# Splitting the first load of a DMA-bound rotation kernel into 2 KB and 62 KB of each row

## Chip, cores and metric

One core of a Trainium2 chip. The metric is the time of one execution on the device in microseconds (us).

## The reference

```python
def reference(x):                       # x: (32, 3, 256, 256) float32
    return np.rot90(x, k=2, axes=(-2, -1)).astype(np.float32)
```

Each of 96 images of 256 x 256 elements is turned by 180 degrees: as a row of 65,536 elements, it is reversed. 25.17 MB are read and 25.17 MB written, and nothing is computed.

## The kernel before

An image is cut into four rows of 16,384 elements (64 KB), and 32 images make a tile of 128 partitions, 8 MB. Three tiles (A, Bt, Ct) hold everything. VectorE mirrors each row in place through a scratch tile T, and the store puts the four rows of an image in reverse order. All transfers are issued on SyncE's one queue.

```python
E = L // 4                  # 16384 elements, 64 KB
J = E // 8
# ... x4, o4: views of input and output; A, Bt, Ct: [128, E]; T: [128, J]

def load(t, g, lo, hi):
    return nc.sync.dma_start(out=t[:, lo:hi], in_=x4[g][:, lo:hi])

def inside(t):
    for lo in range(0, E // 2, J):
        hi = E - lo - J
        copy(T[:, :], back(t, hi, hi + J))
        copy(t[:, hi:hi + J], back(t, lo, lo + J))
        copy(t[:, lo:lo + J], T[:, :])

TAIL = 1536
load(A, 0, 0, E)
load(Bt, 1, 0, E)
body = load(Ct, 2, 0, E - TAIL)
load(Ct, 2, E - TAIL, E)
inside(A)
first = store(A, 0)         # made to wait for `body`: queued while the last strip is on its way
# ... cut: the dependency of `first` on `body`
for g, t in ((1, Bt), (2, Ct)):
    inside(t)
    store(t, g)
```

Of the kernel before, what the change touches and what calls it, by code (L numbers as in the profile page):

```python
# [2 lines left out]

os.environ.setdefault("NEURON_RT_ULTRASERVER_MODE", "4")

# [4 lines left out]


@with_exitstack
def kernel(
    ctx: ExitStack,
    tc: tile.TileContext,
    x: bass.AP,
    out: bass.AP,
):








    nc = tc.nc
    P = 128

    B, C, H, W = x.shape
    L = H * W
    G = 32
    E = L // 4
    J = E // 8

    x4 = x.rearrange("b c h w -> (b c) (h w)").rearrange(
        "(g n) (s e) -> g (n s) e", n=G, s=4)
    o4 = out.rearrange("b c h w -> (b c) (h w)").rearrange(
        "(g n) (s e) -> g n s e", n=G, s=4)  # L40

    pool = ctx.enter_context(tc.tile_pool(name="slots", bufs=1))
    A = pool.tile([P, E], x.dtype, tag="A")
    Bt = pool.tile([P, E], x.dtype, tag="B")
    Ct = pool.tile([P, E], x.dtype, tag="C")
    T = pool.tile([P, J], x.dtype, tag="T")

    def back(t, lo, hi):
        return t[:, hi - 1:(lo - 1 if lo else None):-1]

    def copy(dst, src):
        tc.keep_in_program_order(nc.vector.tensor_copy(out=dst, in_=src))  # L52

    def load(t, g, lo, hi):
        return nc.sync.dma_start(out=t[:, lo:hi], in_=x4[g][:, lo:hi])  # L55

    def store(t, g):
        return nc.sync.dma_start(out=o4[g][:, ::-1, :], in_=t[:, :])
# [6 lines that stand above are left out]
            copy(t[:, lo:lo + J], T[:, :])  # L65

    TAIL = 1536
    load(A, 0, 0, E)
    load(Bt, 1, 0, E)
    body = load(Ct, 2, 0, E - TAIL)  # L70
    load(Ct, 2, E - TAIL, E)
    inside(A)
    first = store(A, 0)
    tc.add_manual_dep(
        first.ins, body.ins.name,
        mybir.DependencyInfo(mybir.DependencyClass.Sync, mybir.DependencyReason.DATA),
        reason="the first store is queued while the last strip is on its way")
# [5 lines that stand above are left out]
# [1 line left out]
_INS = ['x']  # L84
_OUTS = [((32, 3, 256, 256), 'float32')]


# [23 lines left out]
```

## Time and profile before

| | before |
|---|---|
| time, first 3 runs | 122.18 us median (122.0 to 122.47) |
| span of the program in the trace | 120.2 us |
| DMA queue busy | 97.3% |
| VectorE busy | 37% |

The span is shorter than the time by about 1.8 us that lie outside the program. The steady pace is 2.418 us for a row of 64 KB on one of the 16 DMA engines; each engine takes eight rows of a tile, and each row is one packet in the trace. The start is the stretch from the first issue at 0.73 us until all engines run at that pace. The prediction shows the lines.

### The profile page before, as it was taken

The page shows a single profiled execution, that of the slowest core. Times are in us where ns is not written, and L with a number is a line of the kernel's source. Part 1 is how long each engine was busy: PE and PEld are TensorE (multiplying, and loading weights), DVE is VectorE, ACT ScalarE, POOL GpSimd, SP SyncE. Part 2 cuts the span into 40 slices and gives each one's busy share as a digit, 9 for nine tenths or more (in the row PEclk, how much of TensorE's full clock was granted, in tenths as well). Part 3 has the DMA queues.
Part 4 walks back from the last instruction along what each step waited for, and adds up shares of the span by engine and source line. Part 5 has one row for each costly group of instructions (what it writes and reads, how often), then busy time and mean ns, then how long its engine had stood idle before and what let it go on. Part 6 is the DMA issues. An engine that isn't in the chain of part 4 may idle for free.

```text
span 120.2 us, 93 instructions
## 1 busy us (share of the span) xinstructions
DVE 44.2 (37%) x36; POOL 0.2 (0%) x4
## 2 busy tenths in 40 slices
DVE  0000000499995099999059999400000000000000
POOL 0000000000000000000000000000000000000000
DMA  9888988898889779779499888988898889888990
GB/s 349 349 349 371 676 349 349 371 676 349 349 349 698 316 316 632 316 336 613 202 408 698 349 349 349 698 349 349 349 698 349 349 349 698 349 349 349 632 414 0
DMA packets 1008, 50.33 MB, mean 419 GB/s; under 512 B 112, under 2 KB 112, under 8 KB 240
## 3 DMA queue, kind: packets, MB, share of 16 engines
q1 hardware_dynamic: 1008, 50.33, 97.3%
HBM read 25.17 MB, written 25.17 MB: 419 GB/s over the span
## 4 chain that ended last, share of the span: by engine, by line
DMA 34%; DVE 25%; another core or an unknown queue 4%; issue 1%; SPq 0%; DVEq 0%
DMA Bt<-in_x_dram 34%; DVE T L52 8%; DVE Bt L52 8%; DVE Ct L52 8%; SPq L55 0%; DVEq L52 0%
## 5 line engine op out<-in xcount | busy, mean ns | idle before, releaser
L52 DVE COPY T<-A 128x2048 f32<-128x2048 f32 x4 | 4.9, 1227 | 22.6 <-DMA A<-in_x_dram 22.5
L52 DVE COPY T<-Ct 128x2048 f32<-128x2048 f32 x4 | 4.9, 1227 | 4.5 <-DMA Ct<-in_x_dram 4.4
L52 DVE COPY T<-Bt 128x2048 f32<-128x2048 f32 x4 | 4.9, 1227 | 4.4 <-DMA Bt<-in_x_dram 4.3
L52 DVE COPY Bt<-T 128x2048 f32<-128x2048 f32 x4 | 4.9, 1227 | 0.1
L52 DVE COPY A<-T 128x2048 f32<-128x2048 f32 x4 | 4.9, 1227 | 0.1
L52 DVE COPY Ct<-T 128x2048 f32<-128x2048 f32 x4 | 4.9, 1227 | 0.1
L52 DVE COPY A<-A 128x2048 f32<-128x2048 f32 x4 | 4.9, 1227 | 0.1
L52 DVE COPY Bt<-Bt 128x2048 f32<-128x2048 f32 x4 | 4.9, 1227 | 0.1
L52 DVE COPY Ct<-Ct 128x2048 f32<-128x2048 f32 x4 | 4.9, 1226 | 0.1
L95 POOL MEMSET const-uint8-127<- 128x1 uint8 x1 | 0.1, 102 | 0.0
L95 POOL MEMSET const-bfloat16-1.0<- 128x1 bf16 x1 | 0.1, 101 | 0.0
L95 POOL MEMSET const-float32-0.0<- 128x1 f32 x1 | 0.1, 98 | 0.2 <-issue 0.2
L95 POOL MEMSET const-float32-1.0<- 128x1 f32 x1 | 0.1, 98 | 0.0
## 6 DMA issues: line engine op xcount, KB each, us to landing
Ct<-in_x_dram SPq DMA_DIRECT2D x1, 7424.0 KB, 57.7
Ct<-in_x_dram SPq DMA_DIRECT2D x1, 768.0 KB, 59.2
A<-in_x_dram SPq DMA_DIRECT2D x1, 21.8
Bt<-in_x_dram SPq DMA_DIRECT2D x1, 40.7
out_dram<-A SPq DMA_DIRECT2D x1, 21.3
out_dram<-Bt SPq DMA_DIRECT2D x1, 39.9
out_dram<-Ct SPq DMA_DIRECT2D x1, 42.9
```

Source lines behind the costliest of these rows:

```text
L52: tc.keep_in_program_order(nc.vector.tensor_copy(out=dst, in_=src))
L95: nc = _bacc.Bacc("TRN2", target_bir_lowering=False, num_devices=1)
```

## The change

The idea is to give the DMA engines something short first, so that data flows sooner, and to queue the long rest behind it. The short first part of A is called the head below.

```diff
     TAIL = 1536
-    load(A, 0, 0, E)
+    HEAD = 512
+    load(A, 0, 0, HEAD)
+    load(A, 0, HEAD, E)
     load(Bt, 1, 0, E)
```

## The prediction

> **What bounds the kernel now.** I read the page first, because its slices say at once which resource is full.
>
> ```profile
> span 120.2 us, 93 instructions
> DVE 44.2 (37%) x36; POOL 0.2 (0%) x4
> q1 hardware_dynamic: 1008, 50.33, 97.3%
> HBM read 25.17 MB, written 25.17 MB: 419 GB/s over the span
> ```
>
> VectorE works 37% of the span and the one DMA queue 97.3%. All 50.33 MB pass through that queue, loads first and stores after. So the kernel is a stream of transfers, and VectorE's mirror copies lie beside it. The chain of waits names loads and copies, but only because it follows semaphores; the page's DMA row (eights and nines in nearly every slice) says what really is full. Next I read the timeline, to see when the transfers are issued and how much slack VectorE has.
>
> ```profile
> 0.73 0.39 SPq L55 DMA_DIRECT2D A<-in_x_dram  x1
> 1.18 0.42 SPq L55 DMA_DIRECT2D Bt<-in_x_dram  x1
> 1.64 1.01 SPq L55 DMA_DIRECT2D Ct<-in_x_dram  x2
> 22.51 1.23 DVE L52 COPY T<-A 128x2048 f32<-128x2048 f32 x1 [22.51 <-DMA A<-in_x_dram]
> 41.93 1.23 DVE L52 COPY T<-Bt 128x2048 f32<-128x2048 f32 x1 [4.31 <-DMA Bt<-in_x_dram]
> 59.48 0.63 SPq L58 DMA_DIRECT2D out_dram<-A  x1
> 76.51 0.54 SPq L58 DMA_DIRECT2D out_dram<-Ct  x1
> ```
>
> The SyncE queue issues one load each 0.45 us. A's copies start at 22.51 and twelve of them at 1.26 us are done by 37.6, while A's store is issued only at 59.48, held back on purpose until the body of the third load has landed. VectorE therefore has 21.9 us of slack on A, which is the only tile the change touches. Last I read the stretches of the trace around the start and the tail. A packet is counted, with its whole duration, in the stretch in which it starts; so GB/s times length gives the number of packets, and DMA share times length times 16 over that number gives the mean duration of one.
>
> ```profile
> core 0: us, DVE busy (x) POOL busy (x), PEclk, DMA share, GB/s
> 0.70:1.77 1.07, 0.00 (x0) 0.00 (x0) 1.00 0.00 0
> 1.77:2.00 0.23, 0.00 (x0) 0.00 (x0) 1.00 8.50 2849
> 2.00:2.76 0.76, 0.00 (x0) 0.00 (x0) 1.00 1.31 517
> 2.76:4.68 1.92, 0.00 (x0) 0.00 (x0) 1.00 0.00 0
> 4.68:5.30 0.62, 0.00 (x0) 0.00 (x0) 1.00 3.90 1691
> 58.45:60.60 2.15, 0.00 (x0) 0.00 (x0) 1.00 0.86 360
> 118.80:119.20 0.40, 0.00 (x0) 0.00 (x0) 1.00 0.02 0
> ```
>
> From 1.77 to 2.00, 2849 x 0.23 = 655 KB start, ten rows of 64 KB, of 8.50 x 0.23 x 16 / 10 = 3.13 us each; from 2.00 to 2.76 six more, of 2.66 us. These are the first rows of the 16 engines. The second rows start between 4.68 and 5.30 and take 3.90 x 0.62 x 16 / 16 = 2.418 us each, which is the steady pace: 27.1 GB/s an engine, 434 GB/s for all.
>
> The span can now be added up. Every engine moves 48 rows' worth: 48 x 2.418 = 116.06 us. Before the first packet there are 1.77 us. The slowest engine starts its second row at 5.30, so its first row is as good as begun at 5.30 - 2.42 = 2.88, that is 1.11 us after the first packet of all: this is the **ramp**. The last landing is 76.51 + 42.9 = 119.4 (the last store's time to landing on the page), and 0.8 us of ending follow. 1.77 + 1.11 + 116.06 + about 0.2 for the turn from loads to stores + about 0.3 from last packet to landing + 0.8 = 120.2. The measured time is 1.8 to 2.0 us above the span, outside the program.
>
> **What the Trainium skill says.** "DMA: Bandwidth & Descriptors", section "Where 436 GB/s comes from", puts the ceiling of the ports at 435 GB/s. The trace agrees: 434 GB/s in steady stretches, so no rearrangement of the middle has anything to win. The same page, section "Latency and other measured facts", says that a transfer has a least HBM round trip of about 800 ns "regardless of size". The trace has 1.04 us from issue (0.73) to the first packet (1.77), and first rows that are 0.24 to 0.71 us longer than steady ones (2.66 and 3.13 against 2.418); this fits a start-up latency, but does not show whether it depends on the size of the row. Its section "Queues, rings and completion order" says that each engine takes descriptors in ring order and that data descriptors carry no barrier; so the second part of the load can follow the first with no wait for its completion. Its section "Rules for kernel authors" recommends at least 1 MiB per transfer, and says that under 64 KB one pays mostly overhead. The new head is 256 KB, but it is queued ahead of 25 MB, and the trace's own short transfer, the 768 KB tail, ran well: 0.86 x 2.15 / 8 = 0.231 us for a row of 6 KB, where the steady pace gives 0.227.
>
> **The change, part by part.** It removes one load of A with 128 rows of 64 KB, and adds one with 128 rows of 2 KB and one with 128 rows of 62 KB. Bytes stay.
> - Descriptors: 8 more an engine. A row costs 0.231 - 0.227 = 0.004 us beyond its bytes (the tail, just above), so 8 x 0.004 = 0.03 us. One more completion packet an engine: 0.02 x 0.40 = 0.008 us (the stretch at 118.80 has nothing else). Together **+0.04 us**, on the path, as every engine is full.
> - Issue: one more on the SyncE queue, 0.45 us. B and the two parts of C are issued 0.45 us later, at 1.6 to 2.6, while the queue has rows of A until about 22: hidden. The 62 KB part is issued 0.45 us after the head. The head keeps an engine busy for 8 x (0.0756 + 0.004) = 0.64 us, after a latency that it has anyway. 0.64 is more than 0.45, so the second part should be there 0.19 us before the head runs dry: **0 us**.
> - The ramp: a first descriptor of 2 KB in place of one of 64 KB may let data flow sooner, or let an engine open several rows at once during its latency. This, I take it, is the intent. Of the 1.11 us it can take away anything from 0 to all. I hold that most of it is latency or contention of sixteen engines that open at once, which does not know the row's length: engines that start late (six from 2.00 on) show only 0.24 us of excess, with rows just as long. I put in a mean of **-0.15 us**.
> - VectorE: the first copy reads A's last 2048 columns, so it waits for the 62 KB part, and the next copy waits for the head as well, which is long there. It begins at about 22.5 as before. **0 us**.
>
> The sum is 0.04 + 0 - 0.15 + 0 = -0.1 us, from 122.18 to about 122.1.
>
> **The rivals.** First, the ramp belongs to the long descriptor: then short rows fill the pipe at once, half to all of it goes, 0.5 to 1.1 us, and the time is 121.1 to 121.7. For it: early first rows of 3.13 us against 2.418. Against it: the late ones. Chance 0.25. Second, a bubble: if the second part's descriptors reach the engines later than 0.45 us after the head's, engines run dry and pay the latency twice; +0.2 to +0.6, 122.4 to 122.8. For it: the margin is only 0.19 us. Against it: the hand-over from body to tail and from A to B shows no gap. But those were queued tens of us ahead. Chance 0.25. Third, 128 short rows at a pitch of 64 KB collide in memory: the 256 KB then take, say, twice their 0.6 us, 122.8. Against it: the tail's rows have the same pitch and ran at nearly full pace. Chance 0.05. Otherwise nothing moves but the 0.04 us.
>
> **Range and chances.** The three runs before spread from 122.0 to 122.47, so noise is as large as any effect here. All of the ramp gone gives 121.1, a bubble with noise on top 122.9. I predict **122.1 us**, with 121.5 to 122.7 as the range. For faster by 2% it would have to be 119.7, more than twice the whole ramp: chance 0.01. Slower by 2% is 124.6, four bubbles: 0.01. Within 2%: 0.98.
>
> **What would show it.** After the change: about 1.77 us still ahead of the first packet; 128 packets of 2 KB, some 0.08 us each once data flows; engines begin their first 62 KB row within 0.6 us of each other with none idle; A's last part lands at 22.4 to 22.6, B 19.3 us later; the first store is issued at 59.4 to 59.6 and the last landing is at 119.2 to 119.6. Wrong would be: landing of A under 22.1 (the ramp went: rival one), or over 22.8 with a hole between 2 KB and 62 KB packets (rival two), or 2 KB packets well over 0.1 us after the first one of each engine (rival three). The prediction fails altogether if a shift shows in steady rows, which I take to stay at 2.418 us, or if the store's turn at 60.8 changes by itself.

## The result, and the profile after

| | before | after |
|---|---|---|
| time | 122.25 us median (122.0 to 122.47, 6 runs) | 122.22 us median (122.06 to 122.36, 6 runs) |
| span | 120.2 us | 120.3 us |
| first copy of A starts | 22.51 us | 22.50 us |
| store of A is issued | 59.48 us | 59.46 us |

The ratio is 0.9997, with a 95% interval from 0.9983 to 1.0012: the same time. Here and below, a ratio is the mean time of one kernel's runs over that of the other's of the same rounds, so it is not quite the ratio of the quoted medians. Executions over 1.5% slower than the fastest of the same kernel are left out of the means.

The page of the changed kernel, its queue and its two issues of A (KB, then us from issue to landing):

```profile
q1 hardware_dynamic: 1152, 50.33, 97.4%
A<-in_x_dram SPq DMA_DIRECT2D x1, 7936.0 KB, 21.3
A<-in_x_dram SPq DMA_DIRECT2D x1, 256.0 KB, 2.7
```

There are 144 more packets: 128 rows and 16 completions (one packet of 4 bytes with which each engine ends a transfer). Its timeline:

```profile
0.73 0.86 SPq L55 DMA_DIRECT2D A<-in_x_dram  x2
1.63 0.43 SPq L55 DMA_DIRECT2D Bt<-in_x_dram  x1
22.50 1.23 DVE L52 COPY T<-A 128x2048 f32<-128x2048 f32 x1 [22.50 <-DMA A<-in_x_dram]
59.46 0.63 SPq L58 DMA_DIRECT2D out_dram<-A  x1
```

B is issued 0.45 us later, and everything from A's landing on is where it was. So what there is to see lies before 6 us. The stretches of the start, after the change (columns: stretch, its length, DVE, POOL, PEclk, DMA share, GB/s):

```profile
0.70:1.73 1.03, 0.00 (x0) 0.00 (x0) 1.00 0.00 0
1.73:2.50 0.77, 0.00 (x0) 0.00 (x0) 1.00 0.87 199
2.50:2.65 0.15, 0.00 (x0) 0.00 (x0) 1.00 0.91 355
2.65:3.10 0.45, 0.00 (x0) 0.00 (x0) 1.00 6.22 2380
3.10:5.16 2.06, 0.00 (x0) 0.00 (x0) 1.00 0.00 0
5.16:5.77 0.61, 0.00 (x0) 0.00 (x0) 1.00 3.86 1665
```

Read as in the prediction. From 1.73 to 2.50, 199 x 0.77 = 153 KB start, 75 rows of 2 KB, of 0.87 x 0.77 x 16 / 75 = 0.143 us each. From 2.50 on a row takes 0.91 x 0.15 x 16 / 26 = 0.084 us, which is steady. The head therefore loses 75 x 0.059 / 16 = **0.28 us** an engine, where the 64 KB rows before lost 0.54 (the mean of 3.13 and 2.66 over sixteen rows, less 2.418). From 2.65 to 3.10 the sixteen first rows of 62 KB start, with some 27 last rows of the head: 6.22 x 0.45 x 16 = 44.8 us, less 27 x 0.084, are 42.5 us, or 2.66 us a row, where a steady one takes 2.342 (median of all such rows in the trace). That is **0.31 us** too long. What the head gained at the start is lost at the hand-over: 0.28 + 0.31 = 0.59 against 0.54. There is no hole between: by the packets, the first 62 KB rows start 0.02 us in the mean after the head's completions.

The second rows show what this means for the slowest engine. First the stretch of before, closer than in the prediction:

```profile
4.68:5.25 0.57, 0.00 (x0) 0.00 (x0) 1.00 4.24 1840
```

Before, all sixteen second rows have started (1840 x 0.57 = 1049 KB = 16 x 64 KB) by 5.25, and seven more rows of 2.418 follow: 5.25 + 16.93 = 22.2. After, all have by 5.77, and seven rows of 2.342 follow: 5.77 + 16.39 = 22.2. Landing comes some 0.3 us later in both.

### The profile page after: what moved, and what is told of

It is laid out like the page before. It is cut to its first block, busy times and chain, and to the rows that moved or that the text cites. A ratio compares the mean times of both kernels' runs of the same rounds, so it can differ in the third digit from the quotient of the medians.

```text
span 120.3 us, 96 instructions
## 1 busy us (share of the span) xinstructions
DVE 44.2 (37%) x36; POOL 0.2 (0%) x4
## 4 chain that ended last, share of the span: by engine, by line
DMA 33%; DVE 25%; another core or an unknown queue 4%; issue 1%; SPq 1%; DVEq 0%
DMA Bt<-in_x_dram 33%; DVE T L52 8%; DVE Ct L52 8%; DVE Bt L52 8%; SPq L55 1%; DVEq L52 0%
```

## The experiments

"Excess" is the time by which the packets of the start are longer than steady ones of their size, summed and divided by 16 engines, from DMA shares as above or from the packets themselves. "Mean landing" is the mean of the sixteen completions of A's last part in the trace. Every kernel gave the right result.

| kernel | ratio to before (95%) | excess in head, in first long rows | mean landing of A | store of A issued | span |
|---|---|---|---|---|---|
| before, two traces | | none, 0.54 and 0.74 | 22.29, 22.35 | 59.48, 59.62 | 120.2, 120.4 |
| changed, two traces | 0.9997 (0.9983 to 1.0012) | 0.28 and 0.25, 0.31 and 0.23 | 22.29, 22.26 | 59.46, 59.60 | 120.3, 120.5 |
| head8k | 0.9999 (0.9986 to 1.0012) | 0.51, 0.00 | 22.15 | 59.51 | 120.3 |
| head512b | 1.0049 (1.0037 to 1.0061) | none, 0.60 | 22.72 | 60.07 | 120.9 |
| head_act | 1.0015 (0.9999 to 1.0031) | none, 0.64 | 22.56 | 59.56 | 120.3 |
| late | 1.0039 (1.0015 to 1.0063) | 0.25, 0.45 | 22.58 | 60.02 | 120.9 |
| head4k | 1.0038 (1.0022 to 1.0054) | 0.71, 0.01 | 22.69 | 60.21 | 121.0 |
| head2k16 | 1.0011 (0.9997 to 1.0025) | 0.52, 0.03 | 22.50 | 59.82 | 120.6 |
| head2x2k | 1.0167 (1.0141 to 1.0194) | 0.39, 0.23 | 23.62 | 62.13 | 122.9 |
| head3x2k | 1.0206 (1.0192 to 1.0219) | 0.52, 0.35 | 23.50 | 62.29 | 123.1 |
| mid32 | 1.0259 (1.024 to 1.0279) | 0.31, 0.49 | 23.80 | 61.68 | 122.5 |

Each ratio rests on four to six runs; the second traces of the two kernels, and dense4k below, are single runs.

Take the last two columns first. Span less issue of the store is 60.7 to 60.9 us in every row, and from A's last landing on its slowest engine to the store's issue it is 36.8 to 37.0. Once A has landed there, the rest of the kernel follows as a rigid block, and VectorE has no part in it. So each of these times is decided at the start, in the first 6 us (8 in head2x2k, head3x2k and mid32), and there by the slowest engine: head8k has the earliest mean landing, 0.14 us under before, and no gain, since its last engine lands no sooner (its first copy starts at 22.54).

**First set: is the head's gain given back because the second part comes too late?**

head8k, rows of 8 KB in the first part:

```diff
-    HEAD = 512
+    HEAD = 2048
```

> First part of A with rows of 8 KB instead of 2 KB (8 rows an engine: 2.4 us of work), rest 56 KB. Theory 1 (the short rows start sooner, and the gain is given back because the second part comes to the engines too late behind a head of 0.64 us): the second part is there long before, its first rows show no excess, A's last part lands at 22.1 to 22.2 us instead of 22.48, and the time falls by 0.2 to 0.3%. Theory 2 (a ramp that all engines pay at the start whatever the rows are): A lands at 22.4 to 22.55, the excess sits in the first 8 KB rows, ratio 0.999 to 1.001.

No excess at the hand-over, as theory 1 had it. But the head itself lost 0.51 us, as theory 2 had it. The time is theory 2's.

head512b, rows of 512 B, so that the engines run dry:

```diff
-    HEAD = 512
+    HEAD = 128
```

> First part of A with rows of 512 B (8 rows an engine: under 0.2 us of work, less than the 0.45 us between two issues). Theory 1: the engines run dry for about 0.3 us, the first long rows show more excess than the 0.31 us of the 2 KB head, A lands at 22.6 to 22.9, time up by 0.1 to 0.3%. Theory 2: the dry time lies within the ramp, A lands at 22.4 to 22.55, ratio 0.999 to 1.001.

The stretches of the start:

```profile
1.74:2.22 0.48, 0.00 (x0) 0.00 (x0) 1.00 0.44 131
2.22:2.60 0.38, 0.00 (x0) 0.00 (x0) 1.00 5.71 1889
2.60:3.50 0.90, 0.00 (x0) 0.00 (x0) 1.00 0.94 361
```

123 rows of 512 B (131 x 0.48 = 63 KB) take 0.44 x 0.48 x 16 / 123 = 0.027 us each: no excess at all. Then eleven long rows start by 2.60 and five only later, up to 3.5. Their excess is 0.60 us in the mean, 0.74 for the eleven and 0.31 for the five. The dry time is paid, 0.5% in all: theory 1 has the direction, though the slowest landing (23.08 us) and the time went beyond its ranges. A start isn't something that ends by itself after a set time from the first issue.

head_act, the head from another queue:

```diff
-    load(A, 0, 0, HEAD)
+    nc.scalar.dma_start(out=A[:, 0:HEAD], in_=x4[0][:, 0:HEAD])
```

> The 2 KB part is issued from ScalarE's queue, so the 62 KB part is issued on SyncE's queue at about 0.73 us, together with it and not 0.45 us later. Theory 1: the second part is never late, A lands at 22.1 to 22.2, time down by 0.2 to 0.3%. Theory 2: A lands at 22.4 to 22.55, ratio 0.999 to 1.001.

This one didn't test what it was made for. The engines took the long rows first, and the 2 KB rows singly between them, so there was no head: the page says so.

```profile
A<-in_x_dram SPq DMA_DIRECT2D x1, 7936.0 KB, 21.8
A<-in_x_dram ACTq DMA_DIRECT2D x1, 256.0 KB, 22.0
```

Both parts land together. It behaves like the kernel before, with 0.64 us of excess.

late, the second part 0.36 us later still:

```diff
     load(A, 0, 0, HEAD)
+    nc.sync.dma_start(out=T[0:1, 0:1], in_=x4[0][0:1, 0:1])
     load(A, 0, HEAD, E)
```

> A transfer of 4 bytes (into the scratch tile, overwritten later) is issued between the 2 KB and the 62 KB part, so that the latter is issued 0.9 us after the former instead of 0.45. Theory 1 (every delay of the second part is paid): A lands at 22.7 to 22.95, time up by 0.2 to 0.4%. Theory 2 (a ramp that ends by itself at about 2.9 us hides it): A lands at 22.45 to 22.65, ratio 0.999 to 1.0015.

```profile
0.73 0.38 SPq L55 DMA_DIRECT2D A<-in_x_dram  x1
1.17 0.32 SPq L70 DMA_DIRECT2D T<-in_x_dram  x1
1.54 0.35 SPq L55 DMA_DIRECT2D A<-in_x_dram  x1
```

```profile
2.52:3.46 0.94, 0.00 (x0) 0.00 (x0) 1.00 3.35 1222
5.48:6.22 0.74, 0.00 (x0) 0.00 (x0) 1.00 3.17 1373
```

The 62 KB part is issued at 1.54 us instead of 1.18. The sixteen second rows start between 5.48 and 6.22 us, 0.35 us later in the mean than in the changed kernel. The mean landing is 0.30 us later for 0.36 us of delay, the slowest 0.57 (23.05 against 22.48): theory 1, a little above its range. The ratio is 1.0039. One of the six runs, 124.29 us, counts as slow and isn't in it, and the other five spread from 122.23 to 123.32. Only the run of 122.65 was traced; what made two runs longer by 0.7 and 1.6 us isn't known.

**Second set: how long does the head have to be?** The two unchanged kernels were traced again, for the spread.

head4k, rows of 4 KB:

```diff
-    HEAD = 512
+    HEAD = 1024
```

> First part of A with rows of 4 KB (8 rows an engine: 1.25 us of work), rest 60 KB, so that the second part is issued 0.8 us before the first is done. Theory H (hand-over: in the 2 KB version the 0.32 us that the first 62 KB rows take too long is lateness of the second part, and short rows by themselves shorten the ramp): no excess in the first 60 KB rows (under 0.05 us), 0.25 to 0.35 us in the 4 KB rows, mean landing of A's last part 22.0 to 22.1 instead of 22.29. Theory F (fixed ramp: a start costs each engine 0.5 to 0.6 us in sum however its rows are cut, as soon as more than some KB are asked for): 0.45 to 0.6 us in the 4 KB rows, none in the 60 KB rows, mean landing 22.15 to 22.3. Both: ratio 0.998 to 1.001.

Both theories miss. Nothing is lost at the hand-over, but 4 KB rows lose 0.71 us, more than any other head, and the time goes up by 0.4%.

head2k16, sixteen rows of 2 KB an engine in one transfer:

```diff
-    load(A, 0, 0, HEAD)
-    load(A, 0, HEAD, E)
+    def pieces(v):
+        return v[:, 0:4 * HEAD].rearrange("p (k e) -> p k e", e=2 * HEAD)[:, :, 0:HEAD]
+
+    nc.sync.dma_start(out=pieces(A), in_=pieces(x4[0]))
+    load(A, 0, 3 * HEAD, E)
+    load(A, 0, HEAD, 2 * HEAD)
```

> The head has 16 rows of 2 KB an engine in one transfer (columns 0 to 511 and 1024 to 1535), then come 58 KB rows, then the 2 KB rows left out. Rows as short as in the change, but 1.3 us of work before the hand-over. Theory H: 0.25 to 0.3 us of excess in the head as in the change, under 0.05 in the first 58 KB rows, mean landing of all of A 22.0 to 22.15. Theory F: 0.45 to 0.6 us in the head rows, mean landing 22.2 to 22.4. A third theory L (a long row behind short ones pays an opening of its own): about 0.3 us in the first 58 KB rows in spite of the early issue. All: ratio 0.998 to 1.002.

```profile
1.80:2.50 0.70, 0.00 (x0) 0.00 (x0) 1.00 0.96 117
2.50:3.42 0.92, 0.00 (x0) 0.00 (x0) 1.00 0.85 307
```

In these two stretches 178 rows of 2 KB (117 x 0.70 + 307 x 0.92 = 364 KB) take 23.3 us, or 0.131 us each. Theory L falls: the long rows behind the short ones lose only 0.03 us. Theory H falls too: rows of 2 KB lose 0.52 us when 32 KB an engine are asked for at once, against 0.25 to 0.28 when it is 16 KB. Theory F has the excess, but the mean landing, 22.50 us, is later than its 22.2 to 22.4. So the short start in the changed kernel isn't due to short rows alone. That it is due to little being asked for at once fits this and head512b (4 KB an engine lost nothing), but isn't shown: the number of rows and their addresses changed with the amount.

before_again and after_again:

> The kernel before, unchanged: how far the start's numbers come again in a second trace. A lands at 22.4 to 22.6, excess of the first rows 0.5 to 0.57 us in the mean.

> The changed kernel, unchanged: A's last part lands at 22.4 to 22.6; 0.25 to 0.3 us of excess in the 2 KB rows, 0.28 to 0.36 in the first 62 KB rows.

The changed kernel came again nearly as expected (0.25 in the head; 0.23 at the hand-over, a little less). The kernel before had 0.74 us of excess instead of 0.54, outside what was expected, though its mean landing moved by 0.06 only. Its first packets start 0.14 us earlier in the mean (1.94 us against 2.08), so that 0.14 us of the 0.20 are only an earlier start of the count. So the excess of long rows is uncertain by 0.2 us, and landing is the better measure.

**Third set: more small parts, and the pitch.**

head2x2k and head3x2k:

```diff
     load(A, 0, 0, HEAD)
-    load(A, 0, HEAD, E)
+    load(A, 0, HEAD, 2 * HEAD)
+    load(A, 0, 2 * HEAD, E)
```

```diff
-    load(A, 0, 0, HEAD)
-    load(A, 0, HEAD, E)
+    for k in range(3):
+        load(A, 0, k * HEAD, (k + 1) * HEAD)
+    load(A, 0, 3 * HEAD, E)
```

> A comes as 2 KB, 2 KB and 60 KB of each row, three transfers issued 0.45 us apart. Theory R (every transfer reaches its full flow a set time after its own issue, about 1.95 us for long rows as in seven traces so far, about 1.5 us for a small burst of 2 KB rows; what is queued ahead hides it): the second 2 KB part is fully hidden, the long rows flow from about 3.55 us, and A's last part has a mean landing of 22.05 to 22.2 instead of 22.26 to 22.29; time 0 to 0.2% down. Theory F (a start costs 0.5 to 0.6 us in sum however it is cut): mean landing 22.3 to 22.45 as with the head of sixteen 2 KB rows, ratio 1.000 to 1.002.

> A comes as three parts of 2 KB and one of 58 KB of each row. Theory R: all parts but the first hidden, excess in the first 58 KB rows under 0.1 us, mean landing 22.05 to 22.2, time 0 to 0.2% down (little more than with two parts, as each short row costs 0.008 us beyond its bytes). Theory F: mean landing 22.35 to 22.5, ratio 1.000 to 1.002.

Both theories miss by far: 1.7% and 2.1% slower. The stretches of head2x2k show where:

```profile
2.65:3.64 0.99, 0.00 (x0) 0.00 (x0) 1.00 0.93 346
3.64:4.60 0.96, 0.00 (x0) 0.00 (x0) 1.00 1.80 715
4.60:5.80 1.20, 0.00 (x0) 0.00 (x0) 1.00 0.00 0
5.80:6.03 0.23, 0.00 (x0) 0.00 (x0) 1.00 3.55 1336
```

Until 3.64 the second set of 2 KB rows runs at nearly full pace (0.93 x 0.99 x 16 / 167 = 0.088 us a row): theory R is right so far. Then eleven engines get their first 60 KB row by 4.60 (715 x 0.96 = 686 KB, eleven rows and a few short ones), none follows until 5.80, and the other five get theirs at 5.82, 5.84, 6.00, 6.11 and 6.41 us, though the transfer was issued at 1.64. (The last stretch holds three of these; its two other rows, at 5.91 and 5.99, follow on the end of a first row and are second ones.) All engines had ended their short rows by 3.9, so these five stand idle for two microseconds or more, and the kernel's time is theirs. This is rival two of the prediction, a bubble, in a size that it didn't have. In head3x2k fourteen engines have their first 58 KB row by 5.32, one gets it at 6.30, and one at 7.47, behind a third small part that is late there too.

dense4k, one look, for the start alone: 4 KB rows from a contiguous stretch ahead of the kernel before.

```diff
+    nc.sync.dma_start(out=T[:, 0:1024],
+                      in_=x4[0][0:8, :].rearrange("a (b e) -> (a b) e", e=1024))
     load(A, 0, 0, E)
```

> Ahead of the kernel before, a transfer of 128 rows of 4 KB from one contiguous stretch of 512 KB into the scratch tile (overwritten later; for the comparison of the start alone). Rival three (rows at a pitch of 64 KB collide): under 0.4 us of excess in these rows, where the 4 KB head at the pitch of 64 KB had 0.71. If the pitch doesn't matter: 0.6 to 0.8 us. A lands 1.0 to 1.6 us later than in the kernel before either way.

The first stretch of head4k, and then that of dense4k:

```profile
1.74:2.40 0.66, 0.00 (x0) 0.00 (x0) 1.00 1.17 124
```

```profile
1.74:2.40 0.66, 0.00 (x0) 0.00 (x0) 1.00 0.81 205
```

The same transfer but for its addresses: 20 rows of 0.62 us each started with a pitch of 64 KB (1.17 x 0.66 x 16 / 20), and 33 of 0.26 us from contiguous memory. The excess is 0.25 us instead of 0.71. The pitch, the distance from one row's start to the next in memory, matters at the start for 4 KB rows, as rival three had it for those of 2 KB. The run took 123.15 us against 122.29 for the kernel before, 0.9 us more, though its extra 512 KB alone are 1.2 us of steady work. This is one trace against one; head4k's loss of time, though, stands in six runs.

mid32, a middle transfer with as many bytes but a quarter of the rows:

```diff
     load(A, 0, 0, HEAD)
+    nc.sync.dma_start(out=T[0:32, :], in_=x4[0][0:32, 0:2048])
     load(A, 0, HEAD, E)
```

> As with two heads of 2 KB rows, but the middle transfer brings the same 16 KB an engine in 2 rows of 8 KB (32 rows in all, into the scratch tile, overwritten later) instead of 8 rows of 2 KB (128 in all). Theory N (the hole ahead of the third transfer comes from the number of rows queued ahead of it in a short time): no hole, all sixteen long rows start by 4.0 us, A's last part lands at 23.0 to 23.4, as 0.6 us of work was added to the changed kernel. Theory B (it comes because the third transfer is set up while the engines are already in full flow): some long rows start only at 5 to 6 us, and A's last part lands at 24.5 to 25.8.

Neither, strictly. All sixteen long rows have started by 4.7 us, not by 4.0 and not at 5 to 6, and A's last part lands at 24.70, as theory B had it, 2.2 us after the changed kernel's, where the added bytes account for 0.6. This trace is of the fastest run (124.25 us; the median is 125.31). Theory N falls: with few rows ahead the third transfer is late too. That full flow is the cause isn't shown.

## Why the prediction was right, step by step

- **The whole.** 122.1 was predicted and 122.22 measured; the ratio of 0.9997 lies in the middle of "same". That the gain could not exceed the ramp, and that only the first 6 us matter, was right, and the constant stretches from A's landing to the store's issue and from there to the end show it. But the sum was right by luck: two of its steps, the ramp (off by 0.1 to 0.3 us) and the hand-over (off by 0.2 to 0.3), erred in opposite directions, and any effect of this size lies near the noise of the time.
- **Descriptors, +0.04 us.** Undersized. A 2 KB row takes 0.084 us where its bytes are worth 0.0756, so 0.008 us beyond them and not 0.004; eight of them and one completion of 0.009 make 0.08 us. The 0.004 came from a slip: the tail's share was divided by all its 128 rows, but 360 x 2.15 = 774 KB are 126, which gives 0.234 us a row, the figure of the packets too, and so 0.007 beyond its bytes.
- **The ramp, -0.15 us.** Right in direction, undersized, and not for the reason given. The head lost 0.25 to 0.28 us where long rows lost 0.54 to 0.74. That the ramp "does not know the row's length" was only partly right. With rows at a pitch of 64 KB the loss was none with 4 KB asked for at once by an engine, 0.25 to 0.28 with 16 KB, and 0.5 to 0.7 with 32 KB and more; which of amount, rows and addresses sets it isn't shown, and 32 KB in contiguous 4 KB rows lost 0.25 only.
- **The second part is there in time, 0 us.** This step failed in size: 0.23 to 0.31 us were lost at the hand-over. I had reckoned with the time at which a second packet can start, and packets did start at once. What counts is when the transfer is in full flow. Taking from the packets the mean start of the second long rows, less one steady row, less the transfer's issue, gives 1.88 and 1.94 us for the kernel before, 1.97 and 1.99 for the changed one, 2.04 for head512b and 1.95 for late. So in these six traces a long transfer behind an empty or nearly empty queue flows 1.9 to 2.0 us after its **own** issue. The change moves that issue by 0.45 us and the flow by about 0.5; in exchange 2 KB rows worth 8 x 0.0756 = 0.60 us have been brought in, less 0.08 for the extra descriptors. 0.5 - 0.52 is nothing. Where the second part is issued later (late) or less has been brought in (head512b), the sum is a loss of 0.4 to 0.5%, which is the size that rival two gave. With a longer head (8 KB) the hand-over costs nothing, but the head then has a long ramp of its own.
- **VectorE and the later issues, 0 us.** Right: first copy at 22.50 against 22.51, A's store at 59.46 against 59.48.
- **The rivals.** Rival one (the ramp goes) happened only in the head and didn't last. Rival two's cost came in the changed kernel, 0.3 us, but without its hole; the hole came in head512b (0.5 us in the mean between the head's completions and the first long rows), and much larger with three transfers close together. Rival three was given 0.05 because the tail's rows of the same pitch run at pace. That evidence did not carry over to the start: at 4 KB the pitch costs. Its sign, packets of 2 KB well over 0.1 us after each engine's first, was there too, before 2.5 us (up to 0.53 us); whether the pitch causes it wasn't tried at 2 KB. Nor was why the tail doesn't suffer.

**Still open:** why a third transfer issued 0.9 us after the first reaches some engines only at 4 to 6 us. It isn't the number of rows ahead alone (mid32), nor, in the one traced run of late, its place as third alone (its middle transfer is 4 bytes, and the flow came after 1.95 us). But late had two longer runs that weren't traced, and the same may have happened there. Also open is what the 1.9 us consist of.

No version here beats the kernel before.

## What to carry to other kernels

When a transfer is split so that its first piece starts sooner, the rest is issued later, and its own time from issue to full flow runs from there: reckon the gain as the work brought in by the piece less the delay of the rest. Keep the number of transfers ahead of the first long one small, since one piece of 2 KB rows was free here, and two cost 1.7%. In a kernel that one queue fills to 97%, look at the slowest engine's landing in the first microseconds, not at the mean.

## What the Trainium skill lacked or had wrong

- "DMA: Bandwidth & Descriptors", section "Latency and other measured facts", gives about 600 ns to the first byte on this path, but not from where it counts. Here it was 1.01 to 1.08 us from the start of the issue to the first packet, and 0.63 to 0.65 us from the issue's end, in all traces, whatever the length of the first rows; so the figure agrees if it counts from the end.
- No page has the time from issue to full flow of a large load on an empty queue: 1.88 to 2.04 us in the six traces above.
- The same section lists slow row pitches from 512 KiB up, for copies of tiles with 16 KiB rows. Here a pitch of 64 KB cost 0.71 us against 0.25 us for 4 KB rows, at the start only (one trace each).
- No page says that the third of three transfers issued 0.45 us apart can reach part of the engines late: five of sixteen got its first row only at 5.8 us and after, 4.2 us after its issue.
